# A third quadrant block in the first feed-forward network, with more of its sums made by transfers

## The chip, the cores and the metric

The kernel runs on one core of a Trainium2 chip. The metric is the device time of one execution in microseconds. The engines are named as the profile names them: PE is TensorE (PEld its weight loads), DVE is VectorE, ACT is ScalarE, POOL is GpSimd and SP is SyncE, whose queue issues the weight loads.

## The reference, cut to what matters

Two layers, each with a feed-forward network (FFN), a mixer and a second FFN, over 256 rows of 1024 in float32. The FFNs are what the change touches:

```python
D_FF = 2816   # ((8 * 1024 // 3 + 127) // 128) * 128

def swiglu(h, w_gate, w_up, w_down):
    return (jax.nn.silu(h @ w_gate) * (h @ w_up)) @ w_down

for l in range(2):
    f1 = swiglu(rmsnorm(x, g[0]), ffn_w_gate[l, 0], ffn_w_up[l, 0], ffn_w_down[l, 0])
    x = x + 0.5 * rmsnorm(f1, g[1])
    ...   # the mixer: a state-space scan and chunked attention
    f2 = swiglu(rmsnorm(x, g[4]), ffn_w_gate[l, 1], ffn_w_up[l, 1], ffn_w_down[l, 1])
    x = x + 0.5 * rmsnorm(f2, g[5])
```

## The kernel before

**Arithmetic.** Every large product is made of three matmuls of reduced-precision (fp32r) operands. A weight chunk is 128 x 1024 float32 (512 KB). `load` (line 460) brings it into a `raw` buffer through SP's queue, each load after the one before. `halves` (line 466) makes two tiles of it: `wh`, a rounding copy on ScalarE, and `wl`, the rest `raw - wh`, a subtraction on VectorE. The activations are split in the same way, and a chunk is used as x_h wh + x_h wl + x_l wh. The rows are two token tiles of 128 (`t` is 0 or 1). A chunk that both use stands for 12 matmuls of 512 columns.

**Blocks of an FFN.** `ffn` (line 729) goes through the 2816 hidden columns in six blocks (`N_BLK`), 0 to 4 with 512 columns and 5 with 256. A plain block of 512 multiplies gate and up with eight chunks and, with four more, the down projection of the block before (144 matmuls). An FFN has 66 chunks; those of block 1 are 8 to 19, of block 2 20 to 31, of block 3 32 to 43, of block 4 44 to 55; 64 and 65 are the tail, the down projection of block 5. A mixer has 52 chunks.

**Quadrant blocks.** For the blocks named in `SEVEN` (line 31), `seven` (line 637) takes gate and up of both token tiles together as a two by two product, rows by halves of the 1024 inputs on one side, input halves by gate and up on the other, and makes it of seven products in place of eight. Such a block has 132 matmuls. Sums and differences of the activations are made once for each FFN (`sums`, line 611). Those of the weights are made in `seven`, on the four pairs of raw chunks `b11`, `b21`, `b12`, `b22`, in place: `total(1)`, `total(3)`, `total(2)` and `total(4)`, in this order, each for two chunks:

```python
            if k in BY_DMA:
                minus(to)
                for o, r in zip(to, raws):
                    self.add_to(o, r)
            else:
                for o, r in zip(to, raws):
                    self.tt(o, r, o, ALU.subtract)
```

A sum not named in `BY_DMA` is one VectorE subtraction for each chunk. One that is named is a negation in place on ScalarE (`minus`) and a transfer that adds another `raw` buffer to it (`add_to`, line 379: a DMA from SBUF to SBUF with an accumulating add, issued by POOL). `total(2)` works on the `b11` that `total(1)` wrote, after its conversion to the tiles of the fifth product; `total(4)` adds this new `b11` to `b21`. Each operand set is converted by `halves`, 14 tiles in all where a plain block converts eight.

Before the change, blocks 1 and 3 of the first FFN and blocks 1 to 4 of the second are in quadrants, and the sums 3 and 4 go by transfers: 48 of them.

**What sets the order.** All operations are first recorded with their costs and dependences, then placed by a list scheduler (`Graph.schedule`, line 208) that picks by due times, and are emitted in the order of its start times. Each engine and queue then runs its own part in that fixed order. For an accumulating transfer the scheduler has a cost of 0.9 us on POOL and a latency of 8 us (`ADD_LAT`, line 54); loads go one after the other on a DMA resource of their own. `SLOTS` sets the buffers: 12 `raw`, 8 `wh`, 8 `wl`, 33 `blk`, 8 banks `ps`. Three `raw` buffers are also taken by tables of the state-space scan (`constants`, line 769), which live to the end of the layer's mixer, and two more later by `prep` (line 785). Powers for the row scales and some memsets are POOL's other work.

Of the kernel before, what the change touches and what calls it, by code (L numbers as in the profile page):

```python
# [12 lines left out]
F32 = mybir.dt.float32  # L13
# [3 lines left out]
AF = mybir.ActivationFunctionType  # L17
# [10 lines left out]
SP_LR, SP_LI, SP_DT, SP_D, SP_B = 0, 16, 32, 48, 52  # L28

N_BLK = (512, 512, 512, 512, 512, 256)  # L30
SEVEN = (((1, 3), (1, 2, 3, 4)), ((1, 3), (1, 2, 3, 4)))
FFN_CHUNKS = 66
MIX_CHUNKS = 52
LAYER_CHUNKS = 2 * FFN_CHUNKS + MIX_CHUNKS
# [17 lines left out]
DMA_LAT = 2.1  # L52
DMA_RATE = 350e3
ADD_LAT = 8.0
BY_DMA = (3, 4)


class Buf:
# [264 lines left out]
class Kern:  # L323
# [139 lines left out]
            self.last_raw = self.dma(raw[:, s], self.w_d[i][:, s], after=[self.last_raw] if self.last_raw else [])  # L463
        return raw

    def halves(self, raw, parts=(slice(0, 1024),)):
        wh, wl = self.g.buf("wh", [P, 1024], F32R), self.g.buf("wl", [P, 1024], F32R)
        for s in parts:
            self.act(wh[:, s], raw[:, s], AF.Copy)
            self.tt(wl[:, s], raw[:, s], wh[:, s].bitcast(F32), ALU.subtract)  # L470
        return wh, wl

    def weight(self, i):
        if i not in self.ws:
            g = self.g
            keep = (g.stream, g.rank, g.due)
            self.mode("conv" if i >= 6 else "conv0", "main")
            parts = (slice(0, 512), slice(512, 1024)) if i < 2 else (slice(0, 1024),)
            self.ws[i] = self.halves(self.load(i, parts), parts)
            g.stream, g.rank, g.due = keep  # L480
        return self.ws[i]

# [151 lines left out]
        self.mode()  # L634
        return out

    def seven(self, b, xs, rs, s, acc, pend, first):
        i = self.chunk[0]
        assert self.chunk == [i, i]
        self.chunk = [i + 12, i + 12]  # L640
        t0 = i * 2 * TAU - self.saved
        self.saved += 2 * TAU
        for t in range(2):
            for n in range(12):
                self.mark[(t, i + n)] = len(self.g.ops)

        def conv(raws):
            return [self.halves(r) for r in raws]

        self.mode("conv", "main")  # L650
        def minus(raws):
            for r in raws:
                self.act(r, r, AF.Copy, scale=-1.0)

        def total(k, to, raws):
            if k in BY_DMA:
                minus(to)
                for o, r in zip(to, raws):
                    self.add_to(o, r)
# [4 lines that stand above are left out]
        b11 = [self.load(i), self.load(i + 1)]  # L664
        w1 = conv(b11)
        self.weight(i + 2)
        b21 = [self.load(i + 3), self.load(i + 4)]
        w2 = conv(b21)
        b12 = [self.load(i + 5), self.load(i + 6)]
        total(1, b11, b12)  # L670
        w5 = conv(b11)
        b22 = [self.load(i + 7), self.load(i + 8)]
        total(3, b12, b22)
        total(2, b11, b22)
        w6 = conv(b11)
        self.weight(i + 9)
        w7 = conv(b12)
        w3 = conv(b22)
        self.weight(i + 10)
        total(4, b21, b11)  # L680
        w4 = conv(b21)
        self.weight(i + 11)

        def prod(at, bank, a, w, start):
            self.mode("main", "main", t0 + at * TAU)
            pairs = list(zip(self.cols(a[0]), self.cols(a[1])))
            for u in range(2):
                self.mm_two_k(bank, pairs[2 * u:2 * u + 2], w[u], start and u == 0, u == 1, not start)
            self.mode()

        def down(at, c):
            for t in range(2):
                self.mode("main", "main", t0 + (at + t) * TAU)
                self.wide_step(acc[t], pend[t][c], self.weight(i + (2, 9, 10, 11)[c]), first and c == 0)
            self.mode()

        a11, a12 = xs[0].full
        s1, s2, s3, s4, a22 = s
        p1 = self.ps()
        prod(0, p1, a11, w1, True)  # L700
        k1 = self.blk()
        self.act(k1, p1, AF.Copy)
        down(2, 0)
        prod(4, p1, a12, w2, False)
        sil = [self.blk(), self.blk()]
        self.act(sil[0], p1, AF.Silu, scale=rs[0])
        p5, p6 = self.ps(), self.ps()
        prod(6, p5, s1, w5, True)
        prod(8, p6, s2, w6, True)
        u2, u4 = self.blk(), self.blk()  # L710
        self.tt(u2, p6, k1, ALU.add)
        self.tt(u4, p5, u2, ALU.add)
        down(10, 1)
        p7 = self.ps()
        prod(12, p7, s3, w7, True)
        self.tt(u4, p7, u4, ALU.add)
        prod(14, p5, s4, w3, False)
        h = [self.blk(), u4]
        self.tt(h[0], p5, u2, ALU.add)
        self.stt(h[0], h[0], rs[0], sil[0], ALU.mult, ALU.mult)  # L720
        down(16, 2)
        prod(18, p7, a22, w4, False)
        self.tt(u2, p7, u2, ALU.add)
        self.act(sil[1], u2, AF.Silu, scale=rs[1])
        self.stt(h[1], h[1], rs[1], sil[1], ALU.mult, ALU.mult)
        down(20, 3)
        return [self.t_split(h[t], 4) for t in range(2)]

    def ffn(self, l, f, normed):
        ipost = 1 if f == 0 else 5  # L730
        nxt = (l, 2) if f == 0 else (l + 1, 0)
        xs, rs = (list(z) for z in zip(*normed))
        acc = [(self.ps(), self.ps()) for _ in range(2)]
        pend, first, s, pre = None, True, None, [None, None]
        for b, wd in enumerate(N_BLK):
            if b in SEVEN[l][f]:
                if s is None:
                    s = self.sums(xs)
                pend = self.seven(b, xs, rs, s, acc, pend, first)
                first = False  # L740
            else:
                res = []
                for t in range(2):
                    sil, h = self.blk(), self.blk()
                    gb = self.gemm(t, xs[t])
                    if rs[t] is None:
                        rs[t] = self.row_scale(t, [self.g.ops[self.mark[(t, 2)]]])
                    self.act(sil[:, :wd], gb[:, :wd], AF.Silu, scale=rs[t])
                    up = self.gemm(t, xs[t]) if wd == 512 else gb[:, wd:]
                    self.stt(h[:, :wd], up, rs[t], sil[:, :wd], ALU.mult, ALU.mult)  # L750
                    res.append(self.t_split(h, wd // P))
                    if b == len(N_BLK) - 1:
                        pre[t] = self.pre_gain(t, *nxt)
                    if pend is not None:
                        self.gemm_wide(t, acc[t], pend[t], first, False)
                if pend is not None:
                    first = False
                pend = res
            if b == 3:
                self.gain(l, ipost)  # L760
                if nxt[0] < DEPTH:
                    self.gain(*nxt)
# [552 lines left out]
```

## Time and profile before

| | |
|---|---|
| Time, median of 3 runs | 1142.41 us (1142.34 to 1142.91) |
| The profiled execution | 1138.68 us |
| Its span | 1136.9 us |
| Granted TensorE clock over the span | 0.999 |
| Busy: PE, DVE, ACT, POOL | 98%, 85%, 64%, 7% |
| DMA queue of the loads and of the sums, share of 16 engines | 50.5%, 12.1% |

The profile is of one execution; a time in it is counted from the span's start. Matmuls overlap, so a busy PE isn't a measure of how much it could still do. The DMA share is the mean over the core's 16 DMA engines of the time that their packets took. A line number can be a helper's: L370 is any ScalarE activation, L377 any VectorE operation on two tensors, L381 the accumulating transfer, L417 a matmul, L353 a DMA of SP. Names such as `raw` or `wh` stand for all buffers of that kind. In a row, what stands behind "<-" in square brackets or at the end is what ended the idle time.

### The profile page before, as it was taken

What the parts mean: (1) busy time and instruction counts of PE and PEld (TensorE: products, weight loads), DVE (VectorE), ACT (ScalarE), POOL (GpSimd) and SP (SyncE); (2) the same over time, 40 slices, a digit from 0 to 9 for tenths busy, and PEclk for the clock granted to TensorE, in tenths of its full rate; (3) what the DMA queues carried; (4) which work ended last, traced back from release to release, by engine and by line L of the source; (5) the groups of instructions that cost most, each with busy time, mean ns of one, the idle gap of its engine ahead of it and who ended that gap; (6) DMA issues with size and microseconds to landing.
All of it is one profiled execution on the core that took longest, in us unless ns stands there. A gap on an engine that the chain in (4) does not pass through costs nothing.

```text
span 1136.9 us, 15937 instructions
## 1 busy us (share of the span) xinstructions
PE 1114.6 (98%) x5728; PEld 887.0 (78%) x5728; DVE 971.4 (85%) x1418; ACT 732.4 (64%) x1050; POOL 75.0 (7%) x115
## 2 busy tenths in 40 slices
PE   8999999999999999999999999999999999999997
PEld 6778786777788888778888888777777888888886
DVE  7988996796877899999899789967959688999983
ACT  7846565637754687677577565646386456887752
POOL 0101000000000020100020010000000000211000
PEclk9999999999999999999999999999999999999999
DMA  9976844435374656889749677453534655779951
GB/s 344 271 291 145 319 167 154 161 118 180 108 244 169 198 135 204 278 278 277 260 140 281 211 214 283 148 185 131 177 120 146 226 187 165 189 206 278 289 185 37
DMA packets 67183, 230.22 MB, mean 202 GB/s; under 512 B 7840, under 2 KB 8608, under 8 KB 67104
## 3 DMA queue, kind: packets, MB, share of 16 engines
q1 hardware_dynamic: 60192, 204.03, 50.5%
q0 software_dynamic: 6912, 25.17, 12.1%
q8 instruction: 45, 0.74, 0.2%
q14 instruction: 34, 0.28, 0.1%
HBM read 202.96 MB, written 1.05 MB: 179 GB/s over the span
## 4 chain that ended last, share of the span: by engine, by line
PE 80%; DVE 9%; ACT 5%; issue 3%; DMA 2%; SPq 0%; DVEq 0%; POOLq 0%; ACTq 0%
PE ps L417 75%; DVE wl L377 5%; PE ps L431 4%; ACT blk L370 2%; DVE blk L377 2%; DMA raw<-in_wall_dram 2%; ACT wh L370 2%; PE ps L423 1%; DVE raw L377 1%; DVE blk L396 1%; DMA x<-in_x_dram 0%; ACT raw L370 0%; SPq L353 0%; ACT L370 0%; DVE x L396 0%
## 5 line engine op out<-in xcount | busy, mean ns | idle before, releaser
L417 PE MATMUL ps<-wh,blk 128*128 128x512 f32 x2848 | 879.2, 400 | 2.7 <-DVE blk L377 1.9
L417 PEld LDWEIGHTS ps<-wh,blk 128*128 128x128 f32 x2848 | 530.6, 188 | 127.5 <-DVE blk L377 2.4
L370 ACT ACTIVATE wh<-raw 128x1024 fp32r<-128x1024 f32 (+1 forms) x442 | 455.1, 1052 | 261.9 <-PE ps L417 211.3
L377 DVE TENSOR_TENSOR wl<-raw,wh 128x1024 fp32r<-128x1024 f32 (+1 forms) x442 | 525.4, 1222 | 106.6 <-ACT wh L370 105.9
L417 PE MATMUL ps<-wl,blk 128*128 128x512 f32 x1424 | 524.7, 399 | 0.8 <-DVE wl L377 0.8
L417 PEld LDWEIGHTS ps<-wl,blk 128*128 128x128 f32 x1424 | 267.2, 188 | 61.8 <-DVE wl L377 2.5
L370 ACT ACTIVATE blk<-ps 128x512 fp32r<-128x512 f32 (+4 forms) x156 | 85.9, 562 | 72.8 <-PE ps L431 52.1
L377 DVE TENSOR_TENSOR blk<-ps,blk 128x512 fp32r<-128x512 f32 (+2 forms) x164 | 110.3, 678 | 8.3 <-ACT blk L370 8.1
L431 PE MATMUL ps<-ident,blk 128*128 128x128 f32 x432 | 78.8, 275 | 4.0 <-ACT raw L370 4.0
L370 ACT ACTIVATE blk<-blk 32x128 f32<-32x128 f32 (+4 forms) x148 | 59.0, 399 | 21.2 <-DVE blk L377 13.3
L431 PEld LDWEIGHTS ps<-ident,blk 128*128 128x128 f32 x432 | 55.0, 140 | 21.6 <-ACT raw L370 4.7
L381 POOL DMA_DIRECT2D raw<-raw x48 | 41.6, 867 | 340.3 <-ACT raw L370 283.4
L370 ACT ACTIVATE blk<-ps,s 128x512 f32<-128x512 f32 (+1 forms) x68 | 43.6, 654 | 23.5 <-PE ps L417 20.1
L377 DVE TENSOR_TENSOR raw<-raw,raw 128x1024 f32<-128x1024 f32 x48 | 58.4, 1228 | 0.1
L392 POOL TENSOR_TENSOR s<-s,mhalf 128x1 f32<-128x1 f32 x24 | 21.3, 887 | 491.7 <-DVE s L404 491.7
L370 ACT ACTIVATE raw<-raw 128x1024 f32<-128x1024 f32 x48 | 50.2, 1053 | 5.0 <-DVE raw L377 5.0
L377 DVE TENSOR_TENSOR blk<-blk,blk 128x512 f32<-128x512 f32 (+3 forms) x70 | 43.0, 631 | 0.1
L370 ACT ACTIVATE blk<-blk,s 128x128 f32<-128x128 f32 (+2 forms) x76 | 34.6, 486 | 9.0 <-DVE blk L377 8.8
L396 DVE SCALAR_TENSOR_TENSOR blk<-blk,s,blk 128x512 f32<-128x512 f32 x44 | 32.8, 751 | 0.9 <-ACT blk L370 0.8
L377 DVE TENSOR_TENSOR blk<-ps,raw 128x512 f32<-128x512 f32 x32 | 19.8, 682 | 6.8 <-PE ps L417 6.8
L417 PEld LDWEIGHTS ps<-blk,blk 128*32 128x32 f32 (+2 forms) x256 | 15.4, 147 | 12.1 <-issue 9.8
L417 PE MATMUL ps<-blk,blk 128*32 128x32 f32 (+2 forms) x256 | 24.1, 260 | 0.0
(98 smaller groups left out, 401.0 us busy)
## 6 DMA issues: line engine op xcount, KB each, us to landing
raw<-in_wall_dram SPq DMA_DIRECT2D x366, 512.0 KB, 4.9
raw<-raw POOLq DMA_DIRECT2D x48, 512.0 KB, 5.6
gain<-in_gains_dram SPq DMA_DIRECT2D x22, 256.0 KB, 4.3
blk<-in_bias_dram SPq DMA_DIRECT2D x8, 256.0 KB, 5.0
raw<-in_wall_dram SPq DMA_DIRECT2D x4, 256.0 KB, 3.6
blk<-in_sp_dram SPq DMA_DIRECT2D x4, 256.0 KB, 5.5
x<-in_x_dram SPq DMA_DIRECT2D x3, 256.0 KB, 5.5
out_dram<-x SPq DMA_DIRECT2D x2, 256.0 KB, 2.0
```

Source lines behind the costliest of these rows:

```text
L370: self.nc.scalar.activation(out=out.ap(), in_=in_.ap(), func=func, **k)
L377: lambda: self.nc.vector.tensor_tensor(out=out.ap(), in0=a.ap(), in1=b.ap(), op=op))
L381: lambda: self.nc.gpsimd.dma_start(out=out.ap(), in_=in_.ap(), accum_op=ALU.add), func="dma")
L392: lambda: self.nc.gpsimd.tensor_tensor(out=out.ap(), in0=a.ap(), in1=b.ap(), op=ALU.pow))
L396: return self.g.op("dve", cost, [out], [a, s, b], lambda: self.nc.vector.scalar_tensor_tensor(out=out.ap(), in0=a.ap(), scalar=ap(s), in1= ...
L417: return self.g.op("pe", cost, [out], [lhsT, rhs], lambda: self.nc.tensor.matmul(out.ap(), lhsT=lhsT.ap(), rhs=rhs.ap(), start=start, stop ...
L423: self.nc.tensor.matmul(out.ap(), lhsT=lhsT.ap(), rhs=rhs.ap(), start=start, stop=stop)
L431: lambda o=o, s=s: self.nc.tensor.transpose(o.ap(), s.ap(), self.ident.ap()))
```

## The change

Block 2 of the first FFN joins blocks 1 and 3 in both layers. `BY_DMA` is now by FFN: in the first one the sums 2, 3 and 4 go by transfers, in the second still 3 and 4. And for the even chunks 44 to 64 of each layer (`ADDED`, all in the first FFN, from block 4 to the tail) `wl` is made in another way: ScalarE writes -`wh` into it, and an accumulating transfer adds `raw`. The packing of the weights on the host follows `SEVEN`.

```diff
--- before.py
+++ after.py
@@ -28,7 +28,7 @@
 SP_LR, SP_LI, SP_DT, SP_D, SP_B = 0, 16, 32, 48, 52
 
 N_BLK = (512, 512, 512, 512, 512, 256)
-SEVEN = (((1, 3), (1, 2, 3, 4)), ((1, 3), (1, 2, 3, 4)))
+SEVEN = (((1, 2, 3), (1, 2, 3, 4)), ((1, 2, 3), (1, 2, 3, 4)))
 FFN_CHUNKS = 66
 MIX_CHUNKS = 52
 LAYER_CHUNKS = 2 * FFN_CHUNKS + MIX_CHUNKS
@@ -52,7 +52,8 @@
 DMA_LAT = 2.1
 DMA_RATE = 350e3
 ADD_LAT = 8.0
-BY_DMA = (3, 4)
+BY_DMA = ((2, 3, 4), (3, 4))
+ADDED = range(44, 66, 2)
 
 
 class Buf:
@@ -463,8 +464,13 @@
             self.last_raw = self.dma(raw[:, s], self.w_d[i][:, s], after=[self.last_raw] if self.last_raw else [])
         return raw
 
-    def halves(self, raw, parts=(slice(0, 1024),)):
+    def halves(self, raw, parts=(slice(0, 1024),), added=False):
         wh, wl = self.g.buf("wh", [P, 1024], F32R), self.g.buf("wl", [P, 1024], F32R)
+        if added:
+            self.act(wh, raw, AF.Copy)
+            self.act(wl, wh.bitcast(F32), AF.Copy, scale=-1.0)
+            self.add_to(wl.bitcast(F32), raw)
+            return wh, wl
         for s in parts:
             self.act(wh[:, s], raw[:, s], AF.Copy)
             self.tt(wl[:, s], raw[:, s], wh[:, s].bitcast(F32), ALU.subtract)
@@ -476,7 +482,7 @@
             keep = (g.stream, g.rank, g.due)
             self.mode("conv" if i >= 6 else "conv0", "main")
             parts = (slice(0, 512), slice(512, 1024)) if i < 2 else (slice(0, 1024),)
-            self.ws[i] = self.halves(self.load(i, parts), parts)
+            self.ws[i] = self.halves(self.load(i, parts), parts, i % LAYER_CHUNKS in ADDED)
             g.stream, g.rank, g.due = keep
         return self.ws[i]
 
@@ -634,7 +640,7 @@
         self.mode()
         return out
 
-    def seven(self, b, xs, rs, s, acc, pend, first):
+    def seven(self, f, xs, rs, s, acc, pend, first):
         i = self.chunk[0]
         assert self.chunk == [i, i]
         self.chunk = [i + 12, i + 12]
@@ -653,7 +659,7 @@
                 self.act(r, r, AF.Copy, scale=-1.0)
 
         def total(k, to, raws):
-            if k in BY_DMA:
+            if k in BY_DMA[f]:
                 minus(to)
                 for o, r in zip(to, raws):
                     self.add_to(o, r)
@@ -736,7 +742,7 @@
             if b in SEVEN[l][f]:
                 if s is None:
                     s = self.sums(xs)
-                pend = self.seven(b, xs, rs, s, acc, pend, first)
+                pend = self.seven(f, xs, rs, s, acc, pend, first)
                 first = False
             else:
                 res = []
```

## Rows read from the trace of the kernel before

**Rows 1.** The page: busy times by engine; the chain that ended last.

```profile
PE 1114.6 (98%) x5728; PEld 887.0 (78%) x5728; DVE 971.4 (85%) x1418; ACT 732.4 (64%) x1050; POOL 75.0 (7%) x115
...
PE 80%; DVE 9%; ACT 5%; issue 3%; DMA 2%; SPq 0%; DVEq 0%; POOLq 0%; ACTq 0%
```

**Rows 2.** The chain in order of time: start, length, what.

```profile
1040.22 27.83 PE ps L417 x120
```

**Rows 3.** Windows, only what names `wh`: length; PE, PEld, DVE, ACT busy (count).

```profile
32.64:64.33 31.69, 26.40 (x90) 16.29 (x88) 22.84 (x20) 19.07 (x20) 1.00 1.01 308
64.33:99.50 35.17, 30.27 (x96) 17.83 (x96) 14.68 (x13) 12.97 (x13) 1.00 0.62 196
```

**Rows 4.** All instructions: as above, POOL; then clock, DMA share, GB/s.

```profile
32.64:131.37 98.73, 97.73 (x430) 77.96 (x429) 88.91 (x143) 65.54 (x73) 7.67 (x10) 1.00 0.81 258
131.37:203.63 72.26, 70.01 (x369) 54.70 (x368) 59.82 (x131) 40.52 (x69) 3.87 (x10) 1.00 0.53 177
413.82:511.81 97.99, 95.72 (x422) 76.01 (x421) 94.51 (x100) 73.49 (x84) 9.83 (x14) 1.00 0.80 238
596.53:693.63 97.10, 97.10 (x430) 78.34 (x428) 84.01 (x107) 63.85 (x71) 6.16 (x8) 1.00 0.79 249
693.63:765.32 71.69, 69.96 (x370) 54.77 (x368) 59.65 (x131) 40.51 (x69) 3.87 (x10) 1.00 0.52 181
975.40:1069.96 94.56, 94.56 (x422) 76.52 (x420) 94.49 (x101) 75.51 (x86) 9.46 (x11) 1.00 0.86 261
413.82:444.87 31.05, 31.05 (x137) 24.92 (x136) 31.02 (x36) 24.56 (x29) 2.95 (x6) 1.00 0.65 190
444.87:479.22 34.35, 32.87 (x145) 25.66 (x144) 31.93 (x33) 23.75 (x28) 3.29 (x4) 1.00 0.87 260
511.81:542.88 31.07, 31.07 (x137) 25.11 (x136) 31.07 (x35) 23.47 (x26) 2.58 (x3) 1.00 0.94 288
```

**Rows 5.** Groups by line and shape: count, busy us, mean ns, idle before.

```profile
L377 DVE TENSOR_TENSOR wl<-raw,wh 128x1024 fp32r<-128x1024 f32 x438 | 522.7, 1226 | 104.0 <-ACT wh L370 103.3
L370 ACT ACTIVATE wh<-raw 128x1024 fp32r<-128x1024 f32 x438 | 452.6, 1056 | 259.4 <-PE ps L417 211.3 <-issue 23.3 <-DMA raw<-in_wall_dram 18.0
...
L377 DVE TENSOR_TENSOR raw<-raw,raw 128x1024 f32<-128x1024 f32 x48 | 58.4, 1228 | 0.1
...
L377 DVE TENSOR_TENSOR blk<-ps,blk 128x512 f32<-128x512 f32 x80 | 54.9, 692 | 1.6 <-ACT blk L370 1.6
...
L370 ACT ACTIVATE raw<-raw 128x1024 f32<-128x1024 f32 x48 | 50.2, 1053 | 5.0 <-DVE raw L377 5.0
...
L381 POOL DMA_DIRECT2D raw<-raw x48 | 41.6, 867 | 340.3 <-ACT raw L370 283.4 <-DVE raw L377 27.8 <-ACT wh L370 17.2
...
L370 ACT ACTIVATE blk<-ps 128x512 f32<-128x512 f32 x40 | 22.8, 586 | 9.8 <-PE ps L431 5.9 <-PE ps L417 4.0
```

**Rows 6.** Sums' DMA queue (packets, MB, share); windows with sums, with loads.

```profile
q0 software_dynamic: 6912, 25.17, 12.1%
...
40.00:46.00 6.00, 6.00 (x28) 4.84 (x27) 6.00 (x7) 6.00 (x9) 0.87 (x1) 1.00 1.03 205
676.00:684.00 8.00, 8.00 (x36) 6.49 (x35) 7.14 (x18) 5.64 (x6) 0.00 (x0) 1.00 1.02 410
```

**Rows 7.** DMA issues, 32.64 to 203.63 (same count from 596.53 to 765.32).

```profile
raw<-in_wall_dram SPq DMA_DIRECT2D x60, 512.0 KB, 5.0
```

**Rows 8.** POOL's work on `raw`: count, ns, first and last start; landing.

```profile
L358 POOL MEMSET raw<- x6: 117/124/130, 17.2 to 426.3; 128x16 f32 x6
...
DMA to landing us min/median/max: 4.5/5.6/9.1
```

**Rows 9.** Timelines, layer 0, second FFN, block 2: start, length, idle before.

```profile
455.72 0.86 POOL L381 DMA_DIRECT2D raw<-raw  x1 [0.52 <-ACT wh L370]
...
464.46 2.96 ACT L370 ACTIVATE wh<-raw 128x1024 fp32r<-128x1024 f32 x3 [6.78 <-DMA raw<-in_wall_dram]
...
466.84 0.74 PE L417 MATMUL ps<-wl,blk 128*128 128x512 f32 x2 [0.53 <-DVE wl L377]
```

## The prediction

> **What bounds the kernel now.** I read the page first. TensorE is busy for 98% of the span and holds 80% of the chain that ended last; VectorE is at 85%, ScalarE at 64% [rows 1]. Busy time alone proves little where matmuls overlap, so the chain gives the rate: 120 matmuls in 27.83 us, 0.232 us each, at the full granted clock [rows 2]. Next I cut the first and second FFNs into their blocks by counting matmuls: a quadrant block has 132 of 512 columns (88 of them read `wh`), a plain one 144 (96). Two windows, a quadrant block's and a plain one's, show the cut; the two over 88 lie on its edges [rows 3]. The windows of those blocks are the table on which all else rests [rows 4].
>
> Blocks 1 to 3 of a first FFN (quadrant, plain, quadrant) have 408 matmuls, 94.7 us at that rate, and take 98.73 us in layer 0 and 97.10 in layer 1. Blocks 1 to 3 of a second FFN are three quadrant blocks in a row: 396 matmuls, 91.9 us, in 97.99 and 94.56 us. So TensorE is the bound, with 2 to 6 us of transposes and waits in each such stretch. Beside it VectorE is full in the second FFNs (94.5 us of either), and DMA stands at 0.79 to 0.86. The second FFN is thus a measured sample of what the change makes of the first one, except for the transfers.
>
> **Matmuls removed.** A quadrant block does 7 products of 12 matmuls where a plain one does 8. Block 2 of two first FFNs: 24 matmuls x 0.232 = 5.6 us, all on the path. This is the only gain on TensorE; `sums` is already paid for block 1.
>
> **Conversions and sums of block 2, per layer.** Fourteen weight tiles are converted instead of eight: 6 more ScalarE copies of 1.056 and 6 more VectorE subtractions of 1.226. Of the eight half sums, two stay on VectorE (1.228) and six become a ScalarE negation (1.053), a POOL issue (0.867) and a transfer [rows 5]. The outputs take one more ScalarE copy (0.586) and five VectorE additions (0.692).
>
> **Third sum of blocks 1 and 3, per layer.** Four VectorE sums go; four negations and four transfers come. **Even chunks 44 to 64, per layer:** eleven subtractions leave VectorE; eleven negations and eleven transfers come.
>
> Together, per layer: VectorE 6 x 1.226 + 2 x 1.228 + 5 x 0.692 - 4 x 1.228 - 11 x 1.226 = -5.1 us. ScalarE (6 + 0.56 + 21) x 1.055 = +29 us, twenty-one of these being the negations; over the roughly 170 us from block 1 to the tail it goes from 106.1 to 135 us in layer 0 (65.54 + 40.52 before) [rows 4], so it stays covered on average. POOL gets 21 issues, 18 us, on a nearly empty engine; queued behind them are only the row scale's power and the memsets. I cost these three engines at nothing, and price a lost cover below.
>
> **The transfers** are the part that is not covered. 21 per layer, 42 in all, on top of 48. A stretch with hardly anything but such transfers moves 205 GB/s at a DMA share of 1.03; one with loads alone moves 410 at 1.02 [rows 6]. So 0.524 MB cost 1.28 us of all 16 engines as a load and 2.56 as a sum. The page's share gives 0.121 x 1136.9 / 48 = 2.87 for a sum [rows 6]; its packets queue among themselves, so it is an upper bound. I take 2.7. The second FFN bears it out: 36 loads x 1.28 + 12 sums x 2.7 = 78.5 us, and the window of layer 0 shows 0.80 x 97.99 = 78.4 [rows 4].
>
> Now the budget from block 1 to the end of the first FFN. Layer 0: 0.81 x 98.73 + 0.53 x 72.26 = 118.3 us of DMA now; layer 1: 0.79 x 97.10 + 0.52 x 71.69 = 114.0 [rows 4]. Added: 21 x 2.7 = 56.7. Taken off: each stretch issues 60 loads [rows 7], and counted from the start these reach 12 chunks past the FFN's 66; about 8 of these could come later, 8 x 1.28 = 10 us. Left: 165.0 and 160.7 us. TensorE's own length after the change is 170.99 - 2.8 = 168.2 and 168.79 - 2.8 = 166.0. The clean gain needs DMA busy for 97 to 98% of some 165 us on end. The highest share that a quadrant block has in the trace is 0.94, block 4 of layer 0's second FFN [rows 4]; at that share the stretches last 165.0 / 0.94 = 175.5 (+4.5) and 160.7 / 0.94 = 171.0 (+2.2). Sum: +6.7 us.
>
> Why DMA can't simply run ahead: loads wait for `raw` buffers. There are 12; the three memsets at 17.2 us, and three more at 426.3, take three for tables that live to the end of the mixer [rows 8], so both first FFNs, and the second of layer 0, run with nine. A quadrant block holds eight until its last sum has landed. `total(4)` adds `b11`, which `total(2)` wrote: where `total(2)` was two VectorE sums, it is now a landing of 4.5 to 9.1 us [rows 8], and the fourth sum's transfers start behind it. The load of the next chunk, and ScalarE's conversion of it, queue behind that in an order fixed beforehand. What it looks like is in the trace already, with one transfer stage fewer: in block 2 of layer 0's second FFN the last transfer is issued at 455.72, ScalarE then idles 6.78 us for a load, and TensorE waits 0.53 for `wl` [rows 9]. That block took 34.35 us, against 31.05 for the one before it [rows 4].
>
> For the planned order itself, `schedule` gives a sum 8 us of latency but no DMA time, so this crowding is nowhere in its plan.
>
> Bounds. Of the chunks 44 to 64 no row shows a weight tile that waits for a transfer: nothing if its 4.5 to 9.1 us fall within the lead of eight `wh`/`wl` buffers (about 8 x 2.8 = 22 us, less the lag of the second token tile), up to 5 us a layer if half do not; VectorE relief could gain up to 1 us. I take nothing beside the budget. For blocks 1 to 3 the ends are the layer-1 row with twelve buffers, 94.56, and the third rival below.
>
> **Against which time.** The profiled execution took 1138.68 us (span 1136.9 and 1.8 around it); the median of the three runs is 1142.41, 3.7 more. The sum is a difference, so I add it to the median: 1142.4 + 6.7 = 1149.1.
>
> **Rivals.**
> First, the clean gain: DMA keeps up, TensorE stays the bound, 1142.4 - 5.6 = 1136.8. For it: layer 1's second FFN ran at 0.86 with TensorE unbroken; transfers and loads interleave; VectorE is relieved. Against it: it had twelve buffers, and 97% is needed. The Trainium skill, Perfetto Trace Analysis, Identifying the Most-Contended Engine, judges DMA by HBM utilization and not by how busy its engines are; the sums move nothing from HBM, so by that rule DMA has room and this rival is the result. The trace speaks against the rule here: share 1.03 at half the rate of loads [rows 6]. Decides: whether DMA passes 0.95 over a whole FFN.
>
> Second, a draw: three blocks at nine buffers cost what layer 0's second FFN shows, 97.99, which is -0.7 and +0.9 against today, and the rest hides: about 1142.6.
>
> Third, the chain of sums decides, not the budget: `total(4)` lands one pair of transfers later, 2 x 2.7 + 1.8 (4.5 alone less 2.7) = 7.2 us, less two VectorE sums (2.4): 4.8. Block 2 and 3 of each first FFN then take 34.35 + 4.8 = 39.1, three blocks 31.05 + 78.3 = 109.3: +10.6 and +12.2, 1165. It needs every such delay to reach TensorE.
>
> **How the numbers follow.** Forecast (1143 to 1158) 0.48, clean gain 0.20, draw 0.16, chain 0.16. A difference under 0.2%, 2.3 us, can hardly be told from none. Faster 0.21, same 0.15, slower 0.64. The range reaches to the clean gain's edge and the chain's end: 1137.5 to 1165.
>
> **What would show it.** Right: DMA share over 0.9 from block 1 to the tail of both first FFNs; 90 transfers; landings above today's median of 5.6 us; first-FFN blocks 2 and 3 at 32.5 to 36 us; chain entries of DMA and ScalarE there, with the mixers and second FFNs unchanged. Wrong: these blocks at 31 us each and about 5.6 us gone, or the loss in chunks 44 to 64 alone, or a changed mixer, which would mean that the new plan and not the transfers set the time.

## The result, and the profile after

The changed kernel takes 1180.3 us (median of four runs, 1178.32 to 1180.66) against 1142.46 for the one before: a ratio of 1.0323, 95% interval 1.0305 to 1.0341. The direction was forecast, the size was not: 1149.1 was predicted, the range ended at 1165. One execution among the runs below, of e5, took 1813.39 us at a granted clock of 0.557 over its span; it is left out, and e5's blocks are read from e10.

The page of the changed kernel: busy times by engine, the queue of the accumulating transfers, the chain that ended last; under it the core's span and granted clock.

```profile
PE 1129.9 (96%) x5704; PEld 893.6 (76%) x5704; DVE 962.5 (82%) x1414; ACT 782.1 (66%) x1106; POOL 113.9 (10%) x157
...
q0 software_dynamic: 12960, 47.19, 21.6%
...
PE 62%; DMA 12%; DVE 9%; ACT 9%; issue 7%; POOL 1%; SPq 0%; POOLq 0%; DVEq 0%; ACTq 0%
...
core 0: 1178.3 us, clock 0.982
```

Against [rows 1] and [rows 6]: TensorE lost 18 points of the chain, most of them to DMA (2 to 12%), ScalarE (5 to 9%) and issue (3 to 7%); the transfers' share went from 12.1 to 21.6%; the mean clock fell from 0.999 to 0.982. VectorE (85 to 82%) and ScalarE (64 to 66%) have nearly the same busy share as before.

Blocks 1 to 4 of the first FFN in layer 0 and in layer 1, then block 1 to the end of the FFN, in the columns of [rows 4] (length; PE, PEld, DVE, ACT, POOL; clock, DMA share, GB/s). The cuts again come from counting matmuls.

```profile
36.47:76.58 40.11, 34.16 (x137) 26.44 (x136) 33.24 (x44) 28.95 (x33) 6.26 (x7) 0.91 0.94 259
76.58:115.64 39.06, 33.90 (x142) 27.10 (x140) 31.13 (x44) 26.61 (x31) 5.23 (x6) 0.91 0.91 249
115.64:151.33 35.69, 33.60 (x141) 26.57 (x140) 29.71 (x71) 27.60 (x31) 7.07 (x9) 0.95 1.01 270
151.33:195.53 44.20, 39.13 (x157) 29.61 (x156) 29.71 (x88) 28.78 (x49) 7.66 (x11) 0.92 0.92 266
623.17:658.01 34.84, 32.88 (x137) 26.22 (x136) 33.28 (x37) 28.93 (x34) 5.16 (x6) 0.95 0.94 257
658.01:695.64 37.63, 34.07 (x146) 26.94 (x144) 30.72 (x33) 28.23 (x32) 5.17 (x6) 0.95 0.99 276
695.64:731.56 35.92, 32.82 (x137) 26.15 (x136) 30.68 (x83) 26.83 (x31) 7.04 (x9) 0.95 1.02 274
731.56:768.96 37.40, 35.84 (x158) 27.71 (x156) 26.65 (x60) 27.14 (x47) 6.68 (x10) 1.00 0.99 291
...
36.47:230.41 193.94, 175.67 (x786) 136.44 (x785) 143.69 (x271) 131.45 (x170) 30.25 (x41) 0.94 0.91 254
623.17:805.54 182.37, 170.75 (x785) 133.70 (x784) 141.23 (x237) 130.61 (x170) 28.06 (x39) 0.97 0.93 263
```

Blocks 1 to 3 take 114.86 and 108.39 us where they took 98.73 and 97.10; block 4 takes 44.20 and 37.40 where it took 34.71 and 34.80. From block 1 to the mixer: 193.94 against 170.99 and 182.37 against 168.79, together 36.5 of the 41.4 us by which the span grew. The kernel before's block 4, in layer 0 and in layer 1:

```profile
131.37:166.08 34.71, 34.71 (x157) 28.06 (x156) 32.99 (x93) 20.39 (x36) 1.58 (x3) 1.00 0.58 199
693.63:728.43 34.80, 34.80 (x157) 28.05 (x156) 33.49 (x93) 21.04 (x37) 1.57 (x3) 1.00 0.60 206
```

Most of the rest is a later start of block 1 in layer 0 (36.47 against 32.64), which has nothing to do with the change (last section). The mixers and second FFNs are as they were.

**What one of the new stalls is made of.** The chain of waits of the changed kernel in block 1 of layer 0: start, length, what.

```profile
41.96 9.25 DMA raw<-raw
...
51.26 11.40 DMA raw<-in_wall_dram
...
62.75 1.06 ACT wh L371
...
63.84 0.04 DVE wl L378
...
64.98 0.69 DVE blk L378
...
65.81 0.77 PE ps L418
```

A third sum's transfer takes 9.25 us to land. Its landing frees a `raw` buffer; the load that waited for one is issued 0.05 us later and itself takes 11.40 us in the crowded queue. ScalarE converts it (`wh`), VectorE makes `wl`, and only then comes the addition of an output (`blk`, 0.69) for which TensorE has stood 4.36 us. The load is the second chunk of block 2: TensorE needs nothing of it for another ten microseconds. It is just ahead of the addition in VectorE's fixed order.

**What a stall can cost again.** The changed kernel's windows before that stall, in it, after it, and later:

```profile
59.00:61.00 2.00, 2.00 (x10) 1.65 (x9) 0.94 (x1) 1.03 (x1) 0.00 (x0) 1.00 1.02 276
61.45:65.81 4.36, 0.00 (x1) 0.03 (x1) 2.26 (x3) 2.85 (x3) 0.00 (x0) 0.81 1.02 415
65.90:70.90 5.00, 5.00 (x12) 3.94 (x13) 4.85 (x5) 2.13 (x3) 0.00 (x0) 0.50 0.60 157
71.00:75.00 4.00, 4.00 (x19) 3.23 (x18) 4.00 (x5) 3.34 (x4) 0.04 (x1) 1.00 0.92 336
```

After the stall the granted clock is 0.50, 1.2 in place of 2.4 GHz: 12 matmuls in 5.0 us, where 19 fit into 4.0 later. Over the execution (1 - 0.982) x 1178.3 = 21 us of full clock were not granted, against 1 before; that bounds what slow matmuls cost, since TensorE stood still for a part of it. By the rows of the blocks above, some 18 of the 21 us lie in blocks 1 to 4. Not every loss brings it: block 4 of layer 1 grew by 2.60 us at a clock of 1.00.

**Block 4.** ScalarE in the changed kernel's block 4, one row for each layer, and its parameter loads' size and median time to landing; the last row is the kernel before's.

```profile
166.63 1.70 ACT L371 ACTIVATE blk<-blk 64x256 f32<-64x256 f32 x4 [10.70 <-DMA blk<-in_sp_dram]
...
741.97 1.70 ACT L371 ACTIVATE blk<-blk 64x256 f32<-64x256 f32 x4 [7.82 <-DMA blk<-in_sp_dram]
...
blk<-in_sp_dram SPq DMA_DIRECT2D x4, 256.0 KB, 12.2
```

```profile
blk<-in_sp_dram SPq DMA_DIRECT2D x4, 256.0 KB, 5.5
```

ScalarE idles 10.70 and 7.82 us for a load of the state-space parameters, which lands after 12.2 us in place of 5.5. The weight conversions of block 4 stand behind it.

### The profile page after: what moved, and what is told of

Same layout as the page of the kernel before. It is cut to its first block, busy times and chain, and to the rows that moved or that the text cites. A ratio compares the mean times of both kernels' runs of the same rounds, so it can differ in the third digit from the quotient of the medians.

```text
span 1178.3 us, 16040 instructions
## 1 busy us (share of the span) xinstructions
PE 1129.9 (96%) x5704; PEld 893.6 (76%) x5704; DVE 962.5 (82%) x1414; ACT 782.1 (66%) x1106; POOL 113.9 (10%) x157
## 3 DMA queue, kind: packets, MB, share of 16 engines
q0 software_dynamic: 12960, 47.19, 21.6%
HBM read 202.96 MB, written 1.05 MB: 173 GB/s over the span
## 4 chain that ended last, share of the span: by engine, by line
PE 62%; DMA 12%; DVE 9%; ACT 9%; issue 7%; POOL 1%; SPq 0%; POOLq 0%; DVEq 0%; ACTq 0%
PE ps L418 57%; DMA raw<-in_wall_dram 6%; DVE wl L378 4%; ACT wh L371 3%; ACT blk L371 3%; PE ps L432 3%; DMA blk<-in_sp_dram 3%; DMA raw<-raw 2%; DVE blk L378 2%; ACT raw L371 2%; PE ps L424 1%; DVE blk L397 1%; DVE raw L378 1%; DMA wl<-raw 1%; POOL s L393 1%
## 5 line engine op out<-in xcount | busy, mean ns | idle before, releaser
L371 ACT ACTIVATE wh<-raw 128x1024 fp32r<-128x1024 f32 (+1 forms) x454 | 464.9, 1051 | 253.7 <-PE ps L418 198.4
L378 DVE TENSOR_TENSOR wl<-raw,wh 128x1024 fp32r<-128x1024 f32 (+1 forms) x432 | 511.0, 1213 | 141.9 <-ACT wh L371 141.2
L378 DVE TENSOR_TENSOR blk<-ps,blk 128x512 f32<-128x512 f32 (+2 forms) x174 | 116.0, 670 | 19.6 <-ACT blk L371 16.7
L382 POOL DMA_DIRECT2D raw<-raw x68 | 59.0, 868 | 362.9 <-ACT raw L371 189.5
L371 ACT ACTIVATE raw<-raw 128x1024 f32<-128x1024 f32 x68 | 70.1, 1051 | 8.9 <-DVE raw L378 8.8
L378 DVE TENSOR_TENSOR raw<-raw,raw 128x1024 f32<-128x1024 f32 x44 | 52.9, 1214 | 2.0 <-DMA raw<-in_wall_dram 2.0
L382 POOL DMA_DIRECT2D wl<-raw x22 | 19.0, 866 | 115.6 <-ACT wl L371 89.3
## 6 DMA issues: line engine op xcount, KB each, us to landing
blk<-in_sp_dram SPq DMA_DIRECT2D x4, 256.0 KB, 12.2
```

What stands on the lines that cost most here:

```text
L371: self.nc.scalar.activation(out=out.ap(), in_=in_.ap(), func=func, **k)
L378: lambda: self.nc.vector.tensor_tensor(out=out.ap(), in0=a.ap(), in1=b.ap(), op=op))
L382: lambda: self.nc.gpsimd.dma_start(out=out.ap(), in_=in_.ap(), accum_op=ALU.add), func="dma")
```

## The experiments

Three theories. **A, DMA time**: the 16 engines are what ran out, as the prediction's budget says. **B, the chain of sums**: the fourth sum now waits for the landing of the third, the prediction's third rival. **C, the order**: the plan is another one, and that costs, whatever the transfers do. Ratios are to the kernel before on the same chip, with 95% intervals; lengths are from the profiles. In all of them the third sum is `total(2)` and the fourth is `total(4)` (their order is 1, 3, 2, 4).

| Run | Median us | Ratio | Blocks 1 to 3, layer 0, 1 | Block 4, layer 0, 1 |
|---|---|---|---|---|
| before | 1142.46 | 1 | 98.7, 97.1 | 34.7, 34.8 |
| the changed kernel | 1180.3 | 1.0323 (1.0305 to 1.0341) | 114.9, 108.4 | 44.2, 37.4 |
| e1: block 2 alone | 1135.85 | 0.9929 (0.9914 to 0.9944) | 98.6, 97.3 | 34.7, 34.8 |
| e2: block 2, third sums | 1162.0 | 1.0157 (1.0140 to 1.0174) | 113.9, 104.0 | 34.7, 34.8 |
| e3: chunks 44 to 64 alone | 1140.35 | 0.9969 (0.9957 to 0.9981) | 98.1, 97.0 | 35.1, 35.8 |
| e4: third sums alone | 1150.92 | 1.0055 (1.0040 to 1.0070) | 105.9, 98.4 | 34.7, 34.7 |
| e5: half of each transfer | 1134.21 | 0.9918 (0.9896 to 0.9941) | 95.8, 97.6 (e10) | 38.3, 34.8 (e10) |
| e6: 13 `raw` buffers | 1179.62 | 1.0312 (1.0294 to 1.0330) | 113.1, 107.1 | 42.1, 41.2 |
| e7: DMA time in the plan | 1178.68 | 1.0313 (1.0287 to 1.0338) | 106.6, 105.0 | 43.2, 44.2 |
| e8: fourth sum from `b22` | 1169.36 | 1.0226 (1.0202 to 1.0251) | 109.1, 106.4 | 38.5, 39.3 |
| e9: block 2, chunks 44 to 64 | 1161.62 | 1.0154 (1.0125 to 1.0183) | 99.4, 97.4 | 42.3, 44.2 |
| e11: e2, narrow third sums | 1150.48 | 1.0067 (1.0048 to 1.0087) | 105.8, 100.7 | 34.7, 34.8 |
| e13: e9, early parameters | 1144.86 | 1.0019 (1.0004 to 1.0035) | 98.1, 97.4 | 36.0, 36.8 |
| e14: changed, early parameters | 1170.46 | 1.0251 (1.0222 to 1.0279) | 114.0, 111.8 | 37.0, 34.7 |
| e15: e14, DMA time in the plan | 1167.05 | 1.0206 (1.0175 to 1.0237) | 109.0, 106.2 | 41.3, 43.2 |
| e16: e15, latency 11 | 1169.74 | 1.0231 (1.0198 to 1.0264) | 111.8, 102.2 | 41.3, 38.1 |
| e17: e1, DMA time in the plan | 1126.65 | 0.9854 (0.9828 to 0.9880) | 95.7, 95.4 | 34.7, 34.8 |

### The three parts, one by one

e1, block 2 alone:

```diff
-BY_DMA = ((2, 3, 4), (3, 4))
-ADDED = range(44, 66, 2)
+BY_DMA = ((3, 4), (3, 4))
+ADDED = ()
```

> Block 2 of the first FFNs in quadrants and nothing else of the change: sums 3 and 4 by transfers as before, no transfers in chunks 44 to 64; 56 transfers in all. Theory A, DMA time is what ran out: four more transfers a layer leave the first FFN at the second FFN's load (0.8 to 0.87), so 1138 to 1146 us, near the draw of the prediction. Theory B, the fourth sum's wait behind the third's landing: that wait isn't there either, 1138 to 1146. Theory C, the new order of the plan is what costs: most of the 38 us stays, over 1165.

e2 is the change with `ADDED = ()` alone.

> The change without the transfers of chunks 44 to 64: block 2 in quadrants and the third sums by transfers; 68 transfers. A and B both: blocks 1 to 3 lose as in the changed kernel (12.1 us in block 1, 6.2 in block 2, 9.1 in block 3, both layers together), and block 4, where the changed kernel loses 12.1, returns to some 35 us: 1163 to 1172. If block 4's loss is the aftermath of block 3 and not its own transfers: 1175 to 1180.

e3 is the change with the old `SEVEN` and `BY_DMA = ((3, 4), (3, 4))`.

> Only the transfers of chunks 44 to 64, on the old blocks; 70 transfers. A: block 4 rises from a DMA share of 0.6 to about 1.0 but starts with a full lead from a plain block 2: 0 to +5 us, 1142 to 1148. B: no sum waits for another here, no change: 1140 to 1144. If the transfers of block 4 are bad in themselves: +12, 1154.

e4 is the change with the old `SEVEN` and `ADDED = ()`.

> Only the third sum by transfers, in blocks 1 and 3 with a plain block 2 between them; 56 transfers. A: the plain block has DMA time to spare (share 0.62 to 0.64), so only layer 0's block 1, at 1.01 already, pays for its two transfers: +3 to +6 us, 1145 to 1149. B: each of the four quadrant blocks pays the wait of the fourth sum behind the third, 7.2 less 2.4: up to +19, 1150 to 1161.

Blocks 1 to 3 of each layer in e1, then in e2; then blocks 1 and 3 of each layer in e4:

```profile
34.91:133.48 98.57, 95.74 (x417) 75.41 (x416) 95.66 (x102) 73.52 (x83) 11.19 (x14) 1.00 0.89 270
593.84:691.12 97.28, 95.06 (x418) 75.67 (x417) 95.33 (x101) 72.59 (x82) 9.67 (x12) 1.00 0.86 261
```

```profile
34.88:148.79 113.91, 100.55 (x417) 79.52 (x416) 95.02 (x141) 79.87 (x89) 16.82 (x20) 0.93 0.95 267
609.51:713.52 104.01, 95.77 (x417) 75.72 (x416) 93.48 (x119) 79.55 (x90) 14.76 (x18) 1.00 0.98 281
```

```profile
35.47:74.45 38.98, 33.98 (x138) 25.85 (x137) 32.18 (x40) 26.98 (x31) 5.38 (x6) 0.96 1.03 301
109.64:141.38 31.74, 31.07 (x133) 24.64 (x132) 27.64 (x50) 20.85 (x23) 2.74 (x4) 1.00 0.96 308
605.26:637.03 31.77, 31.32 (x138) 25.02 (x137) 31.12 (x34) 25.10 (x30) 2.58 (x3) 1.00 1.03 319
672.23:703.67 31.44, 31.03 (x133) 24.62 (x132) 27.55 (x50) 20.84 (x23) 2.72 (x4) 1.00 0.96 311
```

Block 2 in quadrants is good, and a little better than A and B expected (1135.85; 1138 to 1146 was written): C falls in its plain form. Blocks 1 to 3 themselves are a draw, as the second FFN's 97.99 [rows 4] foretold; what is gained lies in block 5, 26.7 and 29.6 us where a second profile of the kernel before (e12, last section) has 32.5 and 32.7, and the first 31.5 and 30.8; why block 5 gains isn't shown. The third sums cost 26.2 us on top (e2 against e1; 1162.0 is just under the 1163 to 1172 that was written), 22 of them in blocks 1 to 3, where the DMA share goes to 0.95 and 0.98 and, in layer 0, the clock to 0.93. e4 tells A from B where a plain block stands between: only layer 0's block 1 pays (38.98 us; DMA was at 1.01 there without them [rows 3]), the other three take 31 to 32. So the wait of the fourth sum alone costs next to nothing in three blocks of four. The time, 1150.92, is just above A's range and at the lower end of B's (1150 to 1161); it is the blocks that speak against B's price for each of them. They don't bear out A in its plain form either: block 1 of layer 1 has the same DMA share of 1.03 as that of layer 0, and no loss. The chunks 44 to 64 alone are a small gain (1140.35; 1142 to 1148 was written for A, 1140 to 1144 for B).

### Bytes, waits and order

e5, and e10, the same kernel once more, for its profile:

```diff
-                    self.add_to(o, r)
+                    self.add_to(o[:, 0:512], r[:, 0:512])
...
-            self.add_to(wl.bitcast(F32), raw)
+            self.add_to(wl.bitcast(F32)[:, 0:512], raw[:, 0:512])
```

> The changed kernel with each of its 90 accumulating transfers moving only columns 0 to 511 of 1024 (the other half of each such sum is left out): same order, same waits, half the bytes. A, DMA time: a transfer costs 1.35 instead of 2.7, a first FFN's 29 transfers 39 us instead of 78, and the share falls under 0.85: most of the 38 us goes, 1138 to 1152 us. B, the chain of waits: a landing alone only falls from 4.5 to some 3.2 us, and the fourth sum still waits for the third: 1158 to 1170. C, the order: 1175 to 1181.

> The run with half of each transfer (the other half of each such sum is left out) once more, for an undisturbed profile. DMA time: share under 0.9 in the first FFNs, quadrant blocks at 31 to 34 us, block 4 at 35, span about 1132. Were it the waits, the fourth sums' landings would still come some 20 us after the start of the block.

e8:

```diff
-        total(4, b21, b11)
+        total(4, b21, b22)
```

> The changed kernel with the fourth sum adding b22 in place of the b11 that the third sum writes (so the weights of the seventh product differ from the reference's): the same 90 transfers and bytes, but the fourth sum no longer waits for the third's landing. A: unchanged, 1172 to 1181 us. B: blocks 1 to 3 of both first FFNs give back the wait, 10 to 20 us: 1160 to 1170.

e11 is e2 with:

```diff
+                n = 64 if k == 2 else 1024
                 for o, r in zip(to, raws):
-                    self.add_to(o, r)
+                    self.add_to(o[:, 0:n], r[:, 0:n])
```

> As the run without the transfers of chunks 44 to 64 (block 2 in quadrants, third sums by transfers: 1162.0 us), with the third sums' transfers moving 64 of 1024 columns (the rest of these sums is left out): the negations, the issues, the waits and the order stay, nearly all bytes of the third sums go. Bytes: back to block 2 alone, 1134 to 1141 us. The wait of the fourth sum behind a landing (a small transfer still takes some 2 us to land): 1148 to 1158. Order: 1160 to 1164.

Blocks 1 to 3 by layer in e10, then in e8, then in e11:

```profile
36.09:131.91 95.82, 95.21 (x418) 75.56 (x417) 93.97 (x163) 83.59 (x94) 19.38 (x23) 1.00 0.90 261
...
594.78:692.40 97.62, 94.78 (x417) 75.82 (x416) 93.69 (x147) 83.64 (x95) 17.49 (x21) 1.00 0.87 250
```

```profile
36.34:145.40 109.06, 100.30 (x418) 78.76 (x416) 93.66 (x165) 83.23 (x93) 19.21 (x23) 0.95 0.99 274
613.72:720.12 106.40, 97.79 (x418) 76.82 (x417) 93.08 (x145) 83.51 (x94) 16.48 (x19) 0.98 0.95 266
```

```profile
36.18:141.97 105.79, 98.00 (x418) 78.14 (x416) 95.09 (x141) 79.65 (x89) 16.95 (x20) 0.97 0.88 260
602.62:703.28 100.66, 96.77 (x417) 77.17 (x416) 95.16 (x120) 80.24 (x90) 14.86 (x18) 0.98 0.90 267
```

With half the bytes the same 90 transfers, with the same waits in the same order on every engine, give back all 38 us and some 9 more. That is A's side, even below the 1138 to 1152 that was written, and shows that the loss needs the bytes (all sums are halved, the 48 old ones too, so that 90 halves move a little less than 48 whole ones did); e10 took 1136.64 us, in one execution. But the waits and the order are not nothing. Cutting the fourth sum loose (e8) gives back 11 us with all bytes moved, within B's expectation, not A's, though only 7.8 of them in blocks 1 to 3. The plan changed with it, VectorE's order above all, so these 11 us aren't the wait's alone. And taking nearly all bytes from the third sums (e11, in e2's order on every engine) gives back some 11 of their 26, in the range written for the wait (1148 to 1158): the rest stays with the waits and the order, which A had put at nought.

What stays can be seen in the stall taken apart above. First its load and TensorE's wait in e11, then the same load in e10:

```profile
49.96 9.80 DMA raw<-in_wall_dram
...
62.91 0.47 PE L418 MATMUL ps<-wh,blk 128*128 128x512 f32 x1 [3.72 <-DVE blk L378]
```

```profile
raw<-in_wall_dram SPq DMA_DIRECT2D x1, 512.0 KB, 5.5
```

In e11 this third sum lands 3.8 us after its issue in place of 9.25, and the load no longer waits for it; counted from the start of block 1 it is issued only 1.0 us earlier. It still takes 9.80 us beside the other transfers, and TensorE still stands 3.72 us. With half of all bytes the load takes 5.5 us, and TensorE waits 0.18 us there. So in this stall the load's time in the crowded queue and its place ahead of the addition count for more than the landing that freed its buffer. The expectations had A and B as rivals; the loss needs something of both: a transfer is late in a crowded queue, and it costs TensorE where something that it needs stands behind.

### Buffers and the plan

e6: `"raw": 13` and `"blk": 31` in place of 12 and 33 in `SLOTS`.

> The changed kernel with 13 raw buffers and 31 blk buffers in place of 12 and 33: the first FFNs then have ten in place of nine. If DMA idles because loads wait for raw buffers, one more lets one more load run ahead: 5 to 12 us back, 1168 to 1175. If the 16 engines are simply full (A): 1177 to 1182. Fewer blk buffers could cost something in the mixers, which the blocks' times will show apart.

e7, the scheduler (`ADD_DMA` is 2.7):

```diff
             free[e] = o.end
+            if o.func == "dma":
+                free["dma"] = max(free["dma"], o.start) + ADD_DMA
```

> The changed kernel with a scheduler that also charges each accumulating transfer 2.7 us of the DMA resource on which the loads are placed: same work, another order. If the loss is that the plan doesn't see the DMA time and so queues engines behind late transfers: 10 to 25 us back, 1155 to 1170. If the engines are full whatever the order (A in its plain form): 1174 to 1184.

Neither moved the time. One buffer more, at the price of two `blk` buffers, gives nothing back (blocks 1 to 3 are 1.8 and 1.3 us shorter, block 4 2.2 shorter in layer 0 and 3.8 longer in layer 1), against the 5 to 12 us written for loads that wait for buffers. The plan that knows the DMA time does shorten blocks 1 to 3, by 8.3 and 3.4 us, but loses it again behind them, in block 4 of layer 1 (6.8 us) and in block 5 of both layers: the loss moved.

### Block 4

e9 is the change with `BY_DMA = ((3, 4), (3, 4))`.

> The changed kernel without the third sums' transfers: block 2 in quadrants and the transfers of chunks 44 to 64; 78 transfers. Block 2 alone gave 0.9929 of the time before and the chunks alone 0.9969. If what hurts in the changed kernel's block 4 is the lead that blocks 1 to 3 used up (DMA time as a running account), the two gains add here, since blocks 1 to 3 leave the lead whole: 0.988 to 0.993, 1129 to 1136 us. If the chunks' transfers hurt beside any three quadrant blocks: 1140 to 1150.

It missed by far: 1161.62 where both gains were to add. Block 4 loses 7.5 and 9.4 us although blocks 1 to 3 are nearly as short as in e1, and block 5 of layer 0 takes 36.3 us, 31.5 or 32.5 in the two profiles of the kernel before. ScalarE in layer 0's block 4 of e9, and that block in both layers; then the same block in e3, where the chunks' transfers do no harm:

```profile
156.76 0.84 ACT L371 ACTIVATE blk<-blk 64x256 f32<-64x256 f32 x2 [10.58 <-DMA blk<-in_sp_dram]
...
136.36:178.61 42.25, 37.55 (x157) 28.61 (x156) 30.62 (x114) 23.63 (x40) 5.98 (x9) 0.96 0.96 277
711.01:755.22 44.21, 39.26 (x157) 29.48 (x156) 31.18 (x93) 27.95 (x47) 7.77 (x11) 0.92 0.95 276
```

```profile
133.26:168.35 35.09, 34.96 (x157) 27.97 (x156) 28.38 (x66) 27.50 (x47) 6.70 (x10) 1.00 1.04 315
694.93:730.72 35.79, 35.27 (x157) 27.87 (x156) 27.91 (x66) 27.14 (x47) 6.69 (x10) 1.00 1.03 316
```

e3 has the fuller engines (1.04 and 1.03 against 0.96 and 0.95) and no loss. So a full queue isn't enough; e9 has ScalarE idle for 10.58 us at the state-space parameters. e13 (on e9) and e14 (on the changed kernel) move these two loads:

```diff
-        self.dma(bb_in, self.sp_d[l, :, SP_B:SP_B + 512], after)
-        self.dma(cc_in, self.sp_d[l, :, SP_B + 512:SP_B + 1024], after)
+        soon = [self.g.ops[self.mark[(0, l * LAYER_CHUNKS + 32)]]]
+        self.mode("prep", "bulk", (l * LAYER_CHUNKS + 32) * 2 * TAU - self.saved)
+        self.dma(bb_in, self.sp_d[l, :, SP_B:SP_B + 512], soon)
+        self.dma(cc_in, self.sp_d[l, :, SP_B + 512:SP_B + 1024], soon)
+        self.mode("prep", "bulk")
```

> Block 2 in quadrants and the transfers of chunks 44 to 64 (the run of 1161.6 us), with the two loads of the state-space parameters on SP's queue about 16 loads earlier in each layer, well ahead of block 4; nothing else is changed but the order that follows. In that run ScalarE stood 10.6 us (layer 0) and 12.0 us (layer 1) in block 4 at a copy of these parameters, which took 12 to 16 us to land, and the weight conversions queued behind it. If that wait is block 4's loss: block 4 back to 35 to 37 us, 1135 to 1143 in all. If block 4 loses because the 16 engines are full: 1155 to 1163.

> The changed kernel with the same two loads about 16 loads earlier. ScalarE stood 10.7 and 7.8 us at the parameters in its block 4. If that wait is block 4's loss (12.1 us over the two layers): 1165 to 1170, blocks 1 to 3 as slow as before. If full engines: 1175 to 1182, with the same loss at another wait.

Block 4 of e13, both layers:

```profile
133.69:169.72 36.03, 35.23 (x157) 27.87 (x156) 31.70 (x115) 24.66 (x41) 6.12 (x10) 1.00 1.05 311
699.60:736.41 36.81, 35.31 (x157) 27.87 (x156) 30.77 (x94) 27.27 (x47) 7.33 (x11) 1.00 1.04 308
```

At a DMA share of 1.05 and 1.04 block 4 is back at 36.03 and 36.81, and e13 is some 16 us under e9. In the changed kernel the same step gives back 8 to 10 us. Both lie just above the range written for the wait (1144.86 against 1135 to 1143, 1170.46 against 1165 to 1170) and far from the one for full engines. So block 4's loss is ScalarE standing at a parameter load that a crowded queue made late, with the conversions behind it.

### What the order can save

e15 is e14 with e7's edit; e16 is e15 with `ADD_LAT = 11.0`; e17 is e1 with e7's edit.

> The changed kernel with both: the scheduler charges each accumulating transfer 2.7 us of the loads' DMA resource, and the parameter loads come about 16 loads earlier. Planned DMA time alone brought blocks 1 to 3 from 114.9 and 108.4 us to 106.6 and 105.0, and lost it again in block 4 (43 and 44 us) at the parameters. If late loads at the head of ScalarE's and VectorE's fixed order are the cause in both places, the two add: 1160 to 1167. If the 16 engines are full whatever the order: 1170 or more, with the loss at a third place.

> As the run with planned DMA time and early parameters, and the planned latency of an accumulating transfer 11 us in place of 8, nearer to the landings of the changed kernel (up to 11.4). If the plan's too short latency is a further cause: 3 to 10 us under that run. If the engines' time is all that is left: no change, or slower, since buffers are held longer in the plan.

> Block 2 in quadrants alone (1135.9 us, the fastest so far) with the scheduler that charges transfers 2.7 us of DMA: there the DMA share is 0.86 to 0.89 in blocks 1 to 3, so a plan that knows it should change little: 1131 to 1138. If even there late loads stand ahead of TensorE's inputs, 1128 to 1131.

e15 misses its range by a hair (1167.05): blocks 1 to 3 keep e7's gain only in part, and block 4 loses again (41.3 and 43.2). TensorE's longest waits there are 2.08 us at an addition on VectorE (layer 0) and 4.06 at a conversion on ScalarE (layer 1); for the transfers of `wl` themselves it waits 1.15 and 1.32 us. A longer planned latency doesn't help (1169.74). So of the 38 us, the orders tried here save 13; more came back only where bytes or transfers were taken out. e17 is the opposite case. Blocks 1 to 3 of both layers:

```profile
35.11:130.82 95.71, 94.77 (x418) 75.85 (x416) 95.42 (x104) 74.02 (x83) 11.19 (x14) 1.00 0.91 278
587.67:683.08 95.41, 94.67 (x418) 75.69 (x417) 95.38 (x103) 73.06 (x82) 9.67 (x12) 1.00 0.86 264
```

With block 2 in quadrants, no further transfers, and a plan that charges those there are, they take 95.71 and 95.41 us, 3 and 2 less than before the change with 12 fewer matmuls, and the kernel 1126.65 us: 1.5% faster than the one before and better than either range that was written (1131 to 1138; 1128 to 1131 if late loads stood ahead of TensorE's inputs). It beats both kernels of this study. The time speaks for late loads even there, and so do the waits: the longest of TensorE in e1's blocks 1 to 3, 1.77 and 1.48 us at an addition on VectorE, are gone, and none in e17's reaches 1 us. The new order covers the whole kernel, and another 3.5 us come off the second FFN of layer 0.

Still open is how the whole loss of blocks 1 to 3 divides between a landing's wait and the order around it: e8 takes out the wait with all bytes moved, but changes the order too, and only one stall was followed through e11. That a better order could carry all of the change's transfers isn't excluded either.

## Why the prediction was wrong

From block 1 to the end of the first FFNs the forecast had +6.7 us, and +36.5 came. In the prediction's own terms, the step that failed is the quotient that gave these stretches their length, (DMA time - 10 us) / 0.94. The 10 us taken off in each layer are worth 2 x 10 / 0.94 = 21.3 of the 29.8 us that are missing, the share of 0.94 the other 8.5. In kind, the length doesn't follow from the share: blocks run at 1.03 to 1.05 with hardly a loss (e3, e13). Where the loss was followed, in block 4 and in one stall of block 1, it came from late loads standing ahead of TensorE's inputs in ScalarE's and VectorE's fixed order, and these had no price in the sum.

- **Matmuls removed, 5.6 us: right as a count, and as time in these blocks only in e17**, whose blocks 1 to 3 are 3.0 and 1.7 us shorter, with another order too. In e1 these blocks (98.57, 97.28) are the second rival's 97.99 nearly to the letter.
- **VectorE, ScalarE and POOL at nothing: wrong in kind.** Their busy time is covered, as said. Their order is not: they are the place where a late load becomes a TensorE wait. This is where the mechanism failed: the prediction named it for ScalarE ("queue behind that in an order fixed beforehand", [rows 9]) and then gave it no price in the sum.
- **A sum at 2.7 us of the 16 engines: right.** The budget's 118.3 + 56.7 = 175.0 and 114.0 + 56.7 = 170.7 us stand against 0.91 x 193.94 = 176.5 and 0.93 x 182.37 = 169.6 measured.
- **The 10 us taken off: wrong, and the largest part of the miss.** The stretches still issue 60 loads each; nothing was put off into the mixer. The plan, which charges the sums no DMA time, had no reason to.
- **The share of 0.94: wrong as a limit.** The prediction took it for the highest share of any quadrant block, what the engines can reach, and let the stretch follow as a quotient. But its own [rows 3] have a quadrant block at 1.01, block 1 of layer 0. e3 and e13 run block 4 at 1.03 to 1.05, nearly without loss, and blocks of the changed kernel reach 1.01 and 1.02; over the whole stretch they got 0.91 and 0.93. The one stall followed above shows a load that waits for a buffer and a buffer that waits for a landing; a buffer more gave nothing back (e6). 175.0 and 170.7 at the measured shares are 192 and 184 us, near the 193.94 and 182.37 that were measured; but a share that comes out of the waits foretells nothing. 165.0 and 160.7 at 0.94 were the forecast's 175.5 and 171.0.
- **The granted clock: missing from the sum.** Stalls such as the one shown were followed by microseconds at 1.2 GHz; up to 21 us of full clock in all, some 18 of them in blocks 1 to 4.
- **The chunks 44 to 64: nothing beside the budget, bound 5 us a layer.** Block 4 lost 9.5 and 2.6 us. The bound looked at the transfers' own landing against the weight buffers' lead; what was late was a load of the mixer's parameters in the same queue, which the prediction never listed among what shares it.
- **The third rival's mechanism has a part (e8: 11 us, with another order too), its price as a sum over every block doesn't hold** (e4: three of four quadrant blocks pay next to nothing). The first rival drew on the Trainium skill, Perfetto Trace Analysis, Identifying the Most-Contended Engine, which judges DMA by HBM utilization instead of occupancy. By that the change had to be free of DMA cost; but HBM reads stayed at 202.96 MB, and the kernel slowed by 3.2%, as [rows 6] let expect. The share of busy DMA time is no safe gauge either, as e3 and e13 show.
- **The signs to look for** mostly came: 90 transfers, a share over 0.9 (0.91 and 0.93), landings at a median of 6.5 us over the 90 transfers, mixers and second FFNs unchanged. Blocks 2 and 3 were to take 32.5 to 36 us and took 35.7 to 39.1; block 1 of layer 0, not on that list, lost 8.4.

## What to carry to other kernels

A move of work from a busy engine to DMA is paid in the landing times of everything else on the queues, and these come back through engines that run a fixed order: look for the loads that stand at the head of an engine's queue, also those of a later stage, before trusting a budget of bytes. If a planner places the work, let it charge the transfers to the resource they really use (here about 9 us off a kernel that had the engines' time to spare), and try each part of a bundled change alone: of these three, two gained and only the third sums lost by themselves, yet the two gainers together lost 1.5%.

## What the runs showed of the hardware that was not expected

A stall can cost half as much again through the clock: 4.36 us of standing were followed by 5.0 us at a granted clock of 0.50, in which 12 matmuls ran. At the full clock's 0.232 us each [rows 2] they would have taken 2.8 us, so 2.2 were lost. In the profile before, all blocks in [rows 4] show 1.00.

The first power on POOL varied from execution to execution. A second profile of the kernel before (e12, unchanged code) shows it; its POOL row and TensorE's wait, then the POOL row of the first profile:

> The kernel before, unchanged, for a second profile: its profiled execution took 1138.7 us where its timed runs take 1142 to 1146. If the start is what varies: block 0 of layer 0's first FFN at 29 to 31 us in place of 27.4 and all else as it was, near 1143.

```profile
16.65 3.73 POOL L392 TENSOR_TENSOR s<-s,mhalf 128x1 f32<-128x1 f32 x1 [15.18 <-DVE s L404]
...
22.36 0.50 PE L417 MATMUL ps<-wh,blk 128*128 128x512 f32 x1 [1.80 <-ACT blk L370]
```

```profile
16.36 0.85 POOL L392 TENSOR_TENSOR s<-s,mhalf 128x1 f32<-128x1 f32 x1 [14.89 <-DVE s L404]
```

The first row scale's power takes 3.73 us here and 0.85 in the profile on which the prediction rests; TensorE then waits 1.80 us, the granted clock is 0.50 from 23.6 to 26.9 us, and block 1 starts at 36.53 in place of 32.64. This execution took 1145.37 us, the first 1138.68: the 3.7 us between that profile and its median, which the prediction carried along without a reason, are probably of this kind in the main: the long form stands in the profile of the changed kernel and in those of all other runs read here. Against e12 the change's own cost by span is 1178.3 - 1143.6 = 34.7 us.
